# Output projection in pairs of token tiles with seven block products, in a bidirectional RWKV-7 / short-convolution layer

## The chip, the cores and the metric

One of the eight cores of a Trainium2 chip runs the whole kernel. The metric is the device time of one execution in microseconds (us). Five engines work beside each other: TensorE (PE, matrix products), VectorE (DVE), ScalarE (ACT), GpSimd (POOL) and SyncE (SP, whose queue issues the DMAs). Each engine takes its instructions in the order in which they stand in its own row, and an instruction that waits holds back all that stand behind it in that row.

## The reference, cut to what matters

128 context tokens and 2048 latent tokens of width 1024 go through one layer. Group A (512 channels) is RWKV-7 mixing with one scan in each direction, group B (512 channels) a gated short convolution. What the change touches is the end:

```python
    ya, s_final = _wkv(h, r, k, v, s0, lp)
    ya = ya.astype(x.dtype) * jax.nn.silu(g_a)
    yb = b_gate * _short_conv(c_gate * u_conv, lp['conv_w'], is_latent) * jax.nn.silu(g_b)
    u = jnp.concatenate([ya, yb], axis=-1) @ lp['w_out']
    return x + gate * u, s_final
    ...
    y_sample = _rmsnorm(lat, final_g)
```

So each token's 1024 mixed channels are multiplied by the 1024 x 1024 matrix `w_out`, scaled by a gate, added to x and normalised over the 1024 outputs. All is float32.

## The kernel before, in words

The program has three phases on one timeline. Phase 1 makes the input projection, phase 2 the two scans (17 stages; a stage handles one pair of heads and 512 tokens in each direction), phase 3 the output projection. The order of PE, DVE and ACT around the end of the scan is written out by hand as a long list of words, `LATE` (line 766): a word such as `S20@16` names a step and the stage or token tile that it is for, and `main` (line 1386 on) runs the list word by word. The rows of POOL and SP are set by a scheduler.

**Phase 3.** The mixed channels of all tokens lie in DRAM as `scr_mixT` (channel, token). The tokens are cut into 17 tiles of 128, in the order `TILES` (5 to 12, 0, 13 to 16, 1 to 4: the last scan stage finishes the tiles 13 to 16 and 1 to 4). `w_out` is kept in SBUF as eight blocks of 128 rows, four for the convolution's channels (`CONV`) and four for the scan's (`ATT`), each split in a high part `woh` and a low part `wol` (`w_high`, `w_low`). A product of full float32 precision is made of three matmuls in the reduced type fp32r: high by high, high by low, low by high (`products`, line 1499). For each tile the kernel does the following.

- It loads the tile's 8 blocks of 128 channels in two DMAs (`m_load`, line 1479: `mxc`, `mxa`), rounds them to the high part on ACT (`m_high`, line 1490) and subtracts to get the low part on DVE (`m_low`, line 1496: `mlc`, `mla`).
- For each half h of the 1024 outputs it sums 8 blocks x 3 matmuls of 128 x 512 in one PSUM bank: `conv_part` and `att_part` (words `P`, `B`). In matmuls that is 17 tiles x 2 halves x 24 = 816. For the first three tiles (`AHEAD`) the convolution's half is made first, into `psa`, and set aside in `z0` (`ahead`, line 1507, `ahead_out`).
- DVE multiplies the bank by the gate (`gated`, lines 1559 to 1562, word `Z`), POOL adds x (`added`, line 1568, word `G`), ACT squares and sums (`squares`, line 1576, `Q`), DVE adds the two sums (`square_sum`, line 1580, `ss`), ACT takes the root (line 1583, `rt`), DVE the inverse (line 1586, `rc`) and the scaled output (`out`, line 1591, `fo`), which SP stores.

**The end of the scan.** The last stage, 16, has eight state steps for each direction: `state` (line 1220, words `S00` to `S71`: four matmuls `psS<-sv,E`), then `scaled` (line 1246, `sv`: DVE scales the new state and puts it where the next step reads it). So step i+1 needs the `sv` of step i. `outputs` (line 1265) takes the results out, and `finish` normalises them and writes the last quarter of the scan's channels of eight tiles to `scr_mixT`. Before, these steps stand far apart: between two of them are 12 matmuls of the projection of tiles that are ready.

## Time and profile before

| | us |
|---|---|
| median of three runs | 1581.75 (1580.43 to 1589.68) |
| profiled execution, first to last instruction (span) | 1578.3 |
| first matmul of the projection starts | 1371.26 |
| last matmul of the projection starts | 1570.30 |
| granted TensorE clock, mean | 0.982 |

The own device time of the profiled execution is not shown beside its span, so the text takes the median less the span, 3.45 us, for what lies around it. In the profile, "busy" is the time in which an engine executes; "idle before, releaser" is the time that it stood just before an instruction and what ended it. Matmul durations overlap in a pipeline, so the rate is read from how many fit in a stretch and not from one duration. L1568 is line 1568 of the kernel. Tile names stand without their numbers in the profile: `z<-psu,gb` writes a `z` tile from a `psu` bank and the gate.

### The profile page before, as it was taken

The numbers are of one execution on the slowest core, as the hardware profiler recorded it, in microseconds if no ns is written. First come the engines' busy times: TensorE is split into PE (matmuls) and PEld (weight loads), VectorE is DVE, ScalarE is ACT, GpSimd is POOL, SyncE is SP. The second block draws the span as 40 slices with busy tenths as digits, with TensorE's granted clock in tenths as the row PEclk, the third lists the DMA queues.
The fourth block names the chain that finished last, engine by engine and source line by source line (L and its number), as shares of the span: only waits on it lengthen the run. The fifth ranks groups of instructions, "written<-read, shape, count | busy, mean of one in ns | idle before, by whom it ended". The sixth has DMA issues, their size and how long they took to land.

```text
span 1578.3 us, 39371 instructions
## 1 busy us (share of the span) xinstructions
...
## 2 busy tenths in 40 slices
...
GB/s 371 213 174 264 269 270 332 223 223 115 225 220 217 233 226 180 145 116 233 261 218 267 194 125 178 150 188 159 194 192 179 193 163 149 180 142 188 151 143 93
DMA packets 204579, 313.78 MB, mean 199 GB/s; under 512 B 58088, under 2 KB 147560, under 8 KB 190320
## 3 DMA queue, kind: packets, MB, share of 16 engines
...
## 4 chain that ended last, share of the span: by engine, by line
PE 65%; DVE 14%; POOL 7%; issue 5%; DMA 5%; ACT 2%; SPq 0%; ACTq 0%; DVEq 0%; POOLq 0%
POOL zt L1094 4%; PE psu L1503 4%; PE psu L1504 4%; PE psu L1505 4%; PE psE L1189 3%; POOL ztmp L1091 3%; PE mmb L182 2%; PE mmb L184 2%; PE mmb L183 2%; PE psS L1220 2%; PE mmc L182 2%; PE mmc L184 2%; PE mmc L183 2%; PE mmu L182 2%; PE mmu L184 2%
## 5 line engine op out<-in xcount | busy, mean ns | idle before, releaser
L1094 POOL TENSOR_TENSOR zt<-zt,ztmp 128x30 f32<-128x30 f32 (+7 forms) x510 | 215.4, 422 | 39.8
L1091 POOL TENSOR_TENSOR ztmp<-ab,zt 128x60 f32<-128x60 f32 (+7 forms) x255 | 139.4, 547 | 66.7 <-DVE ab L1082 47.0
L410 POOL TENSOR_TENSOR sh<-rawl 128x384 f32<-128x384 f32 (+1 forms) x48 | 47.5, 1007 | 210.1 <-ACT rawl L401 210.1
L1220 PE MATMUL psS<-sv,E 128*64 128x64 f32 x2176 | 104.6, 229 | 12.8 <-DVE sv L1246 7.3
L1220 PEld LDWEIGHTS psS<-sv,E 128*64 128x64 f32 x2176 | 82.8, 137 | 37.9 <-issue 16.3
L1194 DVE TENSOR_TENSOR E<-psE,msk 128x512 f32<-128x512 f32 x136 | 90.6, 683 | 20.0 <-PE psE L1189 18.9
L1568 POOL TENSOR_TENSOR z<-z,x 128x512 f32<-128x512 f32 x32 | 42.7, 1337 | 147.6 <-DVE z L1562 85.7
L1175 ACT ACTIVATE stf<-psX 64x512 f32<-64x512 f32 x136 | 80.3, 590 | 13.1 <-PE psX L1171 10.7
L434 POOL TENSOR_TENSOR hsl<-sq,hsh 128x384 fp32r<-128x384 f32 (+1 forms) x24 | 34.1, 1421 | 129.9 <-ACT hsh L429 121.6
L1246 DVE TENSOR_TENSOR sv<-psS,pc 64x128 f32<-64x128 f32 x254 | 63.7, 271 | 22.4 <-PE psS L1220 21.7
L182 PE MATMUL mmg<-h,w 128*128 128x384 f32 (+1 forms) x216 | 70.8, 328 | 0.0
L183 PE MATMUL mmg<-h,w 128*128 128x384 f32 (+1 forms) x216 | 70.7, 327 | 0.0
L184 PE MATMUL mmg<-h,w 128*128 128x384 f32 (+1 forms) x216 | 70.7, 327 | 0.0
L219 POOL TENSOR_TENSOR hslq<-ssq,hshq 128x384 fp32r<-128x384 f32 (+1 forms) x4 | 4.8, 1202 | 174.2 <-ACT hshq L218 109.6
L182 PE MATMUL mmb<-h,w 128*128 128x384 f32 (+1 forms) x192 | 63.9, 333 | 4.0 <-DMA w<-scr_wsp 4.0
L182 PE MATMUL mmv<-h,w 128*128 128x384 f32 (+1 forms) x192 | 63.1, 329 | 0.9 <-DVE sg L524 0.6
L184 PE MATMUL mmc<-h,w 128*128 128x384 f32 (+1 forms) x192 | 62.8, 327 | 1.0 <-DVE w L154 1.0
L184 PE MATMUL mmb<-h,w 128*128 128x384 f32 (+1 forms) x192 | 63.7, 332 | 0.0
L183 PE MATMUL mmb<-h,w 128*128 128x384 f32 (+1 forms) x192 | 63.6, 331 | 0.0
L182 PE MATMUL mmu<-h,w 128*128 128x384 f32 (+1 forms) x192 | 63.0, 328 | 0.2
L182 PE MATMUL mmc<-h,w 128*128 128x384 f32 (+1 forms) x192 | 63.0, 328 | 0.0
L184 PE MATMUL mmu<-h,w 128*128 128x384 f32 (+1 forms) x192 | 62.9, 328 | 0.0
...
## 6 DMA issues: line engine op xcount, KB each, us to landing
...
wr<-in_win SPq DMA_DIRECT2D x34, 512.0 KB, 8.2
x<-in_x SPq DMA_DIRECT2D x17, 512.0 KB, 3.9
...
```

The source lines that it names most:

```text
L182: T.matmul(ps[:, :n], w[:, 0, k], hh[:, 0, k, :n], start=k == 0, stop=False)
L183: T.matmul(ps[:, :n], w[:, 0, k], hh[:, 1, k, :n], start=False, stop=False)
L184: T.matmul(ps[:, :n], w[:, 1, k], hh[:, 0, k, :n], start=False, stop=k == 7)
L1091: G.tensor_tensor(tv, ab[:, j:j + 2, j + 2:32].unsqueeze(1).broadcast_to((128, kn, 2, n)), zt[:, :kn, j:j + 2].unsqueeze(3).broadcast_to(( ...
L1094: G.tensor_tensor(zt[:, :kn, j + 2:32], zt[:, :kn, j + 2:32], tv[:, :, r], ALU.subtract)
L1175: P.activation(g.fs[64:128, :, hd, e::2], g.ps["X"][e][hr_].rearrange("p a (b t) -> p b a t", b=2), AF.Copy, scale=-1.0)
L1194: V.tensor_tensor(g.E[n][:, k:k + 2].rearrange("p a b c -> p (a b) c"), pe[:].rearrange("p a b c -> p (a b) c"), B.msk[:, ME[g.d]].unsquee ...
L1220: T.matmul(g.sp[i // 4][r, q, hd, :], g.E[n][:, k, hd, r], g.sv[:, u, hd, :], start=True, stop=True)
L1246: V.tensor_tensor(dst, g.sp[i // 4][0:64, q], B.pc[0:64, d, 2 * p:2 * p + 2, c:c + 1].broadcast_to((64, 2, 64)), ALU.mult)
L1503: T.matmul(ps[:], mh[:, n], hi[:, cs], start=start and n == 0, stop=False)
L1504: T.matmul(ps[:], mh[:, n], lo[:, cs], start=False, stop=False)
L1505: T.matmul(ps[:], ml[:, n], hi[:, cs], start=False, stop=stop and n == 3)
```

## The change

**Three tiles** (5, 6, 7) stay as they were (`SINGLE`), and only tile 5 makes its convolution half first, in pieces of three matmuls (`A10` to `A03`). **The other 14 tiles** are taken in seven pairs (`TWO`). The two tiles of a pair (256 tokens) are seen as a 2 x 2 block matrix: two tiles by two halves of the channels (`K1`, `K2`). `w_out` is a 2 x 2 block matrix too: two halves of channels by two halves of outputs. Seven products of blocks with sums before and after (the Winograd form of Strassen's method) replace eight. A block product is 4 blocks x 3 matmuls of 128 x 512, as before. Before, a pair has 8 x 12 = 96 matmuls, now 7 x 12 = 84; in all there are 732 and not 816.

Around the products there is new work.

- *Once* (`vL`, `t1` to `t4`, `tH`, `tD`): `w_out` is loaded a second time in 12 DMAs; DVE makes 16 sums of 128 x 512, ACT rounds 16, and of the 16 low parts DVE makes 8 and POOL 8. Four of the results replace old blocks of `w_out`, which waits for the last matmul of tile 7 that reads them.
- *For each pair*, one pair ahead: a 512 KB load per tile, and seven left operands: a11, a12 and a22 as loaded, and the sums s3, s1, s2, s4 on POOL (`left_sum`), written over the loaded tile; each is rounded on ACT (`H`) and its low part made on DVE (`D`). Before there were four such operands for two tiles.
- *After the products*: ACT copies the first bank (`EX`), DVE makes seven sums of a bank and an SBUF tile (`E2`, `C11`, `E3`, `C22`, `E4`, `C12`, `C21`) and, in four of these words, a multiplication by the gate of two SBUF tiles. Before it was one multiplication straight from the bank for each half tile, four for two tiles. For the last two tiles DVE adds x and the output goes out in halves.

**The scan's last stage** has its state steps next to each other, both directions by turns, with three matmuls of tile 5 between two steps. Some tiles (`sg`, `w`, `q` of one block) get buffers of their own. The left pool of the scan is closed sooner, since the new right operands lie there.

The diff, cut:

```diff
-    AHEAD = TILES[:3]
+    SINGLE = TILES[:3]
+    TWO = [(a, b) for a, b in zip(TILES[3::2], TILES[4::2])]
+    K1, K2 = (0, 1, 4, 5), (2, 3, 6, 7)
...
-            (V if i == TILES[-1] else G).tensor_tensor(zs[i][:, cs], zs[i][:, cs], xs[i][:, cs], ALU.add)
+            (V if i in TILES[-2:] else G).tensor_tensor(zs[i][:, cs], zs[i][:, cs], xs[i][:, cs], ALU.add)
...
+    def again(j):
+        vr = raws["v", j] = K.spare(6 + j % 2, f"wa{j}", F32), K.small("zt", f"wb{j}"), K.small(("Q00", "Q01", "Q10", "Q11")[j], f"wc{j}")
...
+    def right_sum(n):
+        def f(j):
+            o = right_raw(n, j)
+            x, y = {1: (right_raw(3, j), o), 3: (right_raw(2, j), o), 2: (o, right_raw(1, j)), 4: (o, right_raw(2, j))}[n]
+            V.tensor_tensor(o, x, y, ALU.subtract)
+        return f
+
+    def right_high(n):
+        def f(j):
+            P.copy(tw[n][j][0][:], right_raw(n, j))
+        return f
+
+    def right_low(n):
+        def f(j):
+            hi, lo = tw[n][j]
+            (G if n % 2 else V).tensor_tensor(lo[:], right_raw(n, j), hi[:].bitcast(F32), ALU.subtract)
+        return f
+
+    def both_load(q):
+        for t, i in zip("ab", TWO[q]):
+            mx = raws[t, q] = O.r.tile([128, 8, 128], F32, tag="raw", name=f"m{t}{q}", bufs=2)
...
+    def left_sum(n):
+        def f(q):
...
+            x, y, op = dict(s3=("a11", "s1", ALU.subtract), s1=("s1", "a22", ALU.add), s2=("a22", "s3", ALU.subtract),
+                            s4=("a12", "s2", ALU.subtract))[n]
+            G.tensor_tensor(left_raw(n, q), left_raw(x, q), left_raw(y, q), op)
+        return f
...
+    def left_high(n):
+        def f(q):
+            left_tiles(n, q)
+            P.copy(four(lw[n, q][0]), left_raw(n, q))
+        return f
+
+    def left_low(n):
+        def f(q):
+            V.tensor_tensor(four(lw[n, q][1]), left_raw(n, q), four(lw[n, q][0]).bitcast(F32), ALU.subtract)
+        return f
...
+    ORDER = (1, 6, 2, 7, 5, 3, 4)
+
+    def seventh(n):
+        def f(q):
+            c, nm = (q * 7 + ORDER.index(n)) % 4, f"psw{n}_{q}"
+            ps = pss[n, q] = (O.pr if c == 1 else O.pl).tile([128, 512], F32, tag="u", name=nm) if c % 2 else K.bank(nm)
+            mh, ml = lw[LEFT[n], q]
+            for j in range(4):
+                hi, lo = right(n, j)
+                T.matmul(ps[:], mh[:, j], hi, start=j == 0, stop=False)
+                T.matmul(ps[:], mh[:, j], lo, start=False, stop=False)
+                T.matmul(ps[:], ml[:, j], hi, start=False, stop=j == 3)
+        return f
...
+    def plus(n, src, dst, gate=False):
+        def f(q):
+            z, gb = part(q, *dst)
+            V.tensor_tensor(z, pss[n, q][:], part(q, *src)[0], ALU.add)
+            if gate:
+                V.tensor_tensor(z, z, gb, ALU.mult)
+        return f
...
+C11@5 G0@1 Hs2@6 Ds2@6 Q0@1 M5@5 E3@5 Ha12@6 Da12@6 s4@6 M3@5 C22@5 G1@2 Q1@2 E4@5 Hs1@6 Hs3@6 Ds1@6 Ds3@6
+M4@5 C12@5 G1@1 Hs4@6 Ds4@6 Q1@1 ss@1 rt@1 rc@1 fo@1 M1@6 C21@5 G0@2 Ha22@6 Da22@6 Q0@2 ss@2 rt@2 rc@2 fo@2
```

**How the rows move.** Up to the last matmuls `psE` of stage 16 the rows of PE, DVE and ACT hold the same instructions in the same order; SP has eight of the new loads among the scan's.

*DVE at the end of the scan, before* (`psS` is the bank of a state step, `sv` the state scaled for the next step, `E` an operator of a step, `y` the result of the context tokens, `ymn` and `yss` its mean and square sum):

```order
L1246 TENSOR_TENSOR sv_16807<-psS_0_0_17489,pc 64x128
L1265 TENSOR_TENSOR y_17468<-psS_1_0_17236,y_17468 64x512
L1265 TENSOR_TENSOR y_17468<-psS_1_4_17349,y_17468 64x512
L1292 TENSOR_REDUCE ymn_17553<-y_17468 128x8
L1293 SCALAR_TENSOR_TENSOR y_17468<-ymn_17553,y_17468 128x512
L1194 TENSOR_TENSOR E_1738_17441<-psE_16_1739_17443,msk 128x512
L1301 TENSOR_REDUCE yss_17575<-w_17573 128x8
L1246 TENSOR_TENSOR sv_17018<-psS_1_0_17497,pc 64x128
L1194 TENSOR_TENSOR E_1740_17452<-psE_16_1745_17506,msk 128x512
```

*DVE at the same place, now:*

```order
L1252 TENSOR_TENSOR sv_16807<-psS_0_0_17501,pc 64x128
L1200 TENSOR_TENSOR E_1738_17441<-psE_16_1739_17443,msk 128x512
L1252 TENSOR_TENSOR sv_17018<-psS_1_0_17509,pc 64x128
L1200 TENSOR_TENSOR E_1740_17452<-psE_16_1745_17518,msk 128x512
L1271 TENSOR_TENSOR y_17480<-psS_1_0_17236,y_17480 64x512
L1271 TENSOR_TENSOR y_17480<-psS_1_4_17349,y_17480 64x512
L1298 TENSOR_REDUCE ymn_17567<-y_17480 128x8
L1299 SCALAR_TENSOR_TENSOR y_17480<-ymn_17567,y_17480 128x512
L1252 TENSOR_TENSOR sv_16807<-psS_0_0_17501,pc 64x128
L1252 TENSOR_TENSOR sv_17018<-psS_1_0_17509,pc 64x128
```

The two operators moved ahead of the four instructions on `y`, and the second state of both directions follows right behind them.

*DVE in the projection, before, one token tile* (`z` is the tile's result, `psu` its bank, `mlc` and `mla` the low parts of a coming tile, `ss` the square sum):

```order
L1562 TENSOR_TENSOR z_18700<-psu_0_18645,gb 128x512
L1496 TENSOR_TENSOR mlc_18716<-mxc_18643,mhc_18715 128x512
L1496 TENSOR_TENSOR mla_18738<-mxa_18663,mha_18737 128x512
L1562 TENSOR_TENSOR z_18700<-psu_1_18687,gb 128x512
L1580 TENSOR_TENSOR ss_18718<-ss_18718 128x1
L1586 RECIPROCAL ss_18718<-ss_18718 128x1
L1591 SCALAR_TENSOR_TENSOR z_18700<-z_18700,ss_18718,fg 128x1024
```

*DVE in the projection, now, a stretch of the second pair* (`zw` are the results of its two tiles, `psw` a bank of a block product; `s2r` holds s2, `ma` and `mb` the loaded tiles of the third pair, `mls` and `mla` low parts of its left operands). It begins with the word `C11` and ends before the last low part of s4:

```order
L1728 TENSOR_TENSOR zw_18252<-psw_1_18255,zw_18253 128x512
L1730 TENSOR_TENSOR zw_18252<-zw_18252,gb 128x512
L1689 TENSOR_TENSOR mls_2_18294<-s2r_18275,mhs_2_18293 128x512
L1728 TENSOR_TENSOR zw_18253<-psw_1_18277,zw_18252 128x512
L1689 TENSOR_TENSOR mla_2_18315<-ma_18231,mha_2_18314 128x512
L1728 TENSOR_TENSOR zw_18253<-psw_1_18300,zw_18253 128x512
L1730 TENSOR_TENSOR zw_18253<-zw_18253,gb 128x512
L1728 TENSOR_TENSOR zw_18252<-psw_1_18300,zw_18252 128x512
L1689 TENSOR_TENSOR mls_2_18340<-mb_18233,mhs_2_18339 128x512
L1689 TENSOR_TENSOR mls_2_18343<-ma_18231,mhs_2_18342 128x512
L1728 TENSOR_TENSOR zw_18252<-psw_1_18319,zw_18252 128x512
L1730 TENSOR_TENSOR zw_18252<-zw_18252,gb 128x512
```

The sums of a pair and the low parts for the next pair stand by turns in one row, and behind this stretch come `ss`, the reciprocal and the output of each tile, with the sum of the seventh product between the two tiles.

*POOL in the same pair, now* (before, POOL has only the two additions of x for each tile there):

```order
L1673 TENSOR_TENSOR ma_18231<-ma_18231,mb_18233 128x2x256
L1673 TENSOR_TENSOR mb_18233<-mb_18233 128x2x256
L1673 TENSOR_TENSOR s2r_18275<-mb_18233,ma_18231 128x512
L1591 TENSOR_TENSOR zw_18252<-zw_18252,x_18237 128x512
L1673 TENSOR_TENSOR ma_18231<-ma_18231,s2r_18275 128x2x256
L1591 TENSOR_TENSOR zw_18253<-zw_18253,x_18235 128x512
L1591 TENSOR_TENSOR zw_18252<-zw_18252,x_18237 128x512
L1591 TENSOR_TENSOR zw_18253<-zw_18253,x_18235 128x512
```

The three sums s3, s1 and s2 stand ahead of the first addition of x, and s4 between the first and the second. On ACT the squares of a half tile stand ahead of the roundings of a12 and of s1 for the next pair.

More of the change, by code (lines that the diff above doesn't have):

```diff
@@ L1417, in main, with small, bank @@
         O.pS.close()
-        for p in (O.l0, O.rI, O.r0):
+        for p in (O.rI, O.r0):
             p.close()
-    K.early, K.main, K.spare = early, main, spare
+    def small(tag, name, dt=F32):
+        return (O.rI if tag in ("zt", "dg") else O.r0).tile([128, 512], dt, tag=tag, name=name, bufs=2 if tag == "zt" else 1)
+    def bank(name):
+        return O.pS.tile([128, 512], F32, tag="S", name=name)
+    K.early, K.main, K.spare, K.small, K.bank = early, main, spare, small, bank
 def layout2(I):
@@ L1539, in f @@
         def f(i):
-            ps = pss[h, i] = getattr(O, pool).tile([128, 512], F32, tag="u", name=f"psu{i}_{h}")
+            nm = f"psu{i}_{h}"
+            ps = pss[h, i] = K.bank(nm) if pool == "pS" else getattr(O, pool).tile([128, 512], F32, tag="u", name=nm)
             if i not in z0:
@@ new lines, in left_tiles @@
+    def left_tiles(n, q):
+        x = dict(a11="a", a12="a", a22="c").get(n)
+        pool, b = ((O.r, 1) if x == "c" else (O.l, 2)) if x else (O.w, 1)
+        lw[n, q] = [pool.tile([128, 4, 128], F32R, tag=f"m{m}{x or n}", name=f"m{m}{n}_{q}", bufs=b) for m in "hl"]
+        return lw[n, q]
+    def left_sum(n):
+        def f(q):
+            if n == "s2":
+                raws["s2", q] = K.small("msk", f"s2r{q}")
+            x, y, op = dict(s3=("a11", "s1", ALU.subtract), s1=("s1", "a22", ALU.add), s2=("a22", "s3", ALU.subtract),
+                            s4=("a12", "s2", ALU.subtract))[n]
+            G.tensor_tensor(left_raw(n, q), left_raw(x, q), left_raw(y, q), op)
+        return f
```

147 lines of the change are left out of this document (101 added, 46 removed).

## The prediction

> **What bounds the kernel now.** I read the stages first, then what PE waited for, then the tail. The stages (start and end, length, busy time of PE, PEld, DVE, ACT and POOL with their instructions, granted clock, DMA share, GB/s):
>
> ```profile
> 1340.00:1380.00 40.00, 34.10 (x547) 27.88 (x544) 28.45 (x54) 23.14 (x38) 9.49 (x5) 0.97 0.58 171
> 1500.00:1540.00 40.00, 40.00 (x176) 32.85 (x175) 14.92 (x25) 10.51 (x25) 9.43 (x8) 1.00 0.42 138
> ```
>
> In the second, PE is busy without a gap while DVE works 14.92 of 40 us: 176 matmuls in 40.00 us are 0.2273 us each, 2.73 for a block product of 12. The waits of PE from 1384 to 1571 and the two ends of the projection:
>
> ```profile
> PE psa L1503 <- ACT mhc L1490: 2.1, 1, 2.1
> ...
> 1371.26 0.50 PE L1503 MATMUL psa<-woh,mhc 128*128 128x512 f32 x1
> ...
> 1570.30 0.39 PE L1505 MATMUL psu<-woh,mla 128*128 128x512 f32 x1
> ...
> 1573.71 1.42 DVE L1591 SCALAR_TENSOR_TENSOR z<-z,ss,fg 128x512 f32<-128x512 f32 x2
> ```
>
> One wait of 2.1 us in 199: PE alone sets the pace. DVE's last instruction ends at 1575.13, the span 3.2 us later.
>
> **What the change removes.** 816 matmuls become 732; 84 x 0.2273 = 19.1 us of PE, 2.73 for each pair (21.8 before, 19.1 now). This is the whole gain, 1.2% of 1578. Everything else that the change does costs time, if it isn't hidden under PE.
>
> **The vector engines in a pair.** The groups from 1430 us on (busy, mean ns | idle before):
>
> ```profile
> L1591 DVE SCALAR_TENSOR_TENSOR z<-z,ss,fg 128x1024 f32<-128x1024 f32 (+1 forms) x16 | 20.9, 1312 | 1.4
> L1562 DVE TENSOR_TENSOR z<-psu,gb 128x512 f32<-128x512 f32 x26 | 17.7, 685 | 13.8 <-PE psu L1505 8.4 <-DMA out_y<-z 5.3
> L1496 DVE TENSOR_TENSOR mlc<-mxc,mhc 128x512 fp32r<-128x512 f32 x12 | 8.3, 690 | 17.8 <-ACT mhc L1490 15.7 <-PE psT L1317 2.0
> L1580 DVE TENSOR_TENSOR ss<-ss 128x1 f32<-128x1 f32 x13 | 2.0, 157 | 20.1 <-ACT sq L1576 20.0
> ...
> L1490 ACT CAST mhc<-mxc 128x512 fp32r<-128x512 f32 x12 | 7.4, 620 | 37.0 <-PE psu L1504 37.0
> ...
> L1568 POOL TENSOR_TENSOR z<-z,x 128x512 f32<-128x512 f32 x24 | 31.5, 1314 | 105.2 <-DVE z L1562 84.5 <-DMA mxa<-scr_mixT 13.2 <-DVE ss L1580 5.2
> ```
>
> DVE's work for a pair, now: 7 sums from a bank, 4 multiplications by the gate and 7 low parts, 18 at about 0.69 = 12.4; two outputs at 1.29 = 2.6; four small ones at 0.16 = 0.6. Together 15.6 us, under PE's 19.1. If that were all, the change would gain. But DVE takes its row in order, and the row holds five places where it must wait for a chain over other engines. The price of such a chain stands in the last but one tile:
>
> ```profile
> 1559.74 0.69 DVE L1562 TENSOR_TENSOR z<-psu,gb 128x512 f32<-128x512 f32 x1 [1.39 <-PE psu L1505]
> 1560.51 1.29 POOL L1568 TENSOR_TENSOR z<-z,x 128x512 f32<-128x512 f32 x1 [4.16 <-DVE z L1562]
> 1561.83 0.64 ACT L1576 ACTIVATE sq<-z 128x512 f32<-128x512 f32 x1 [4.21 <-POOL z L1568]
> 1562.37 0.18 ACT L1576 ACTIVATION_READ_ACCUMULATOR sq<-z 128x1 f32 x1
> 1562.59 0.16 DVE L1580 TENSOR_TENSOR ss<-ss 128x1 f32<-128x1 f32 x1 [2.16 <-ACT sq L1576]
> 1562.78 0.29 ACT L1583 ACTIVATE ss<-ss,eps 128x1 f32<-128x1 f32 x1 [0.23 <-DVE ss L1580]
> 1563.11 0.16 DVE L1586 RECIPROCAL ss<-ss 128x1 f32<-128x1 f32 x1 [0.36 <-ACT ss L1583]
> 1563.38 1.29 DVE L1591 SCALAR_TENSOR_TENSOR z<-z,ss,fg 128x1024 f32<-128x1024 f32 x1
> ```
>
> DVE ends the gate at 1560.43 and can start the output at 1563.38: 2.95 us, in which it stood for 2.16 before `ss`. Before, this comes under 10.9 us of PE for each tile and costs nothing. The five waits of a pair, in the order of DVE's row:
>
> - Low part of s2. s3 is written over a11, so it waits for DVE's low part of a11; then POOL makes s3, s1 and s2 (3 x 1.29) and ACT rounds (0.62): 4.65 with the handovers. DVE has `C11` (1.4) in between and stands 3.2.
> - Low part of a12: its rounding stands on ACT behind the square of a half tile, 0.5.
> - Low part of s1: its rounding stands behind a square that waits for POOL's addition behind `C22`: 1.29 + 0.8 + 0.62 + 0.1 = 2.8, less `E4` 0.7: 2.1.
> - `ss` of the first tile: 2.95 less the low part of s4 (0.69) and the small ones (0.3): 1.95. `ss` of the second: 1.95 again.
>
> These are 9.7 us, so DVE needs 15.6 + 9.7 = **25.3 us for a pair** with no instruction slowed. Two things come on top. First, DVE and POOL get in each other's way:
>
> ```profile
> 1417.62 1.29 POOL L1568 TENSOR_TENSOR z<-z,x 128x512 f32<-128x512 f32 x1 [11.50 <-DVE z L1560]
> 1418.03 1.43 DVE L1560 TENSOR_TENSOR z<-z,gb 128x512 f32<-128x512 f32 x1
> ...
> 1420.18 0.67 DVE L1562 TENSOR_TENSOR z<-psu,gb 128x512 f32<-128x512 f32 x1
> ...
> 1421.84 1.36 DVE L1496 TENSOR_TENSOR mla<-mxa,mha 128x512 fp32r<-128x512 f32 x1
> ...
> 1488.72 2.33 DVE L1591 SCALAR_TENSOR_TENSOR z<-z,ss,fg 128x1024 f32<-128x1024 f32 x1
> ```
>
> A DVE instruction on two SBUF tiles that meets a POOL instruction ends 0.55 us after POOL's end (1418.91, 1419.46), and so takes 1.43 or 1.36 and not 0.69, the output 2.33 and not 1.29; one on a bank and one SBUF tile takes 0.67 beside POOL all the same. In a pair the gates, low parts and outputs are of the first kind and POOL has eight instructions and not four. Where two meet (the gates of `C11` and `C22`, the low part of s2, the last addition of either tile) 0.5 to 0.75 us are lost, of which some fall into waits: +1.6 a pair, from 0 to 2.5. The Trainium skill states this as a rule: by its page "SBUF — State Buffer", section "Who interferes with whom", DVE with two SBUF inputs and a GpSimd instruction that reads SBUF exclude each other for a whole instruction, whichever is first. By that rule a pair is 27 us and without it 25.3; the rows above agree with it (1.43 against 0.67).
>
> Second, the loads. On SP's queue the second tile of the pair after next stands behind a load of x that waits for POOL's last addition of this pair, about 3 us before DVE's next pair begins:
>
> ```profile
> x<-in_x SPq DMA_DIRECT2D x11, 512.0 KB, 3.4
> ```
>
> s3 needs the tile 1.4 us into that pair, so 4.4 us are there: one load is in time, two behind each other are late by up to 1.8. I count 0.1: **27.0 us a pair, from 25.3 to 29**. PE's 19.1 lie under it: its products of a pair need the low parts that DVE made a pair before, so PE follows DVE's row and is idle for about 8 us of 27. The eight banks don't hold it up; each is emptied before its next product is due.
>
> **The scan's end.** PE's own work from 1371.26 to the first product of tile 5 with the scan's channels is 24 matmuls (5.5), 56 of state steps (0.45 for 8: 3.2) and four transposes (0.6): 9.3 us. What the steps wait for stands in DVE's row:
>
> ```profile
> 1372.11 1.40 DVE L1265 TENSOR_TENSOR y<-psS,y 64x512 f32<-64x512 f32 x2
> 1373.54 0.69 DVE L1292 TENSOR_REDUCE ymn<-y 128x8 f32<-128x512 f32 x1
> 1374.26 0.69 DVE L1293 SCALAR_TENSOR_TENSOR y<-ymn,y 128x512 f32<-128x512 f32 x1
> ...
> 1376.30 0.27 DVE L1246 TENSOR_TENSOR sv<-psS,pc 64x128 f32<-64x128 f32 x1
> ```
>
> The third step stands behind the four `y` instructions (2.8 us) and finds about 0.3 of cover: 2.5. Each later step needs its `sv` (0.27 twice), and DVE has 9 longer instructions between them against 0.68 of matmuls a step: 3 us more. So 14.8, until 1386.0; from 9.3 to 18.
>
> **From there to the first sum of the first pair.** DVE has 64 instructions in its row: 53 of about 0.70 (37.1), three outputs (3.9), eight small ones (1.4): 42.4 us. They contain the 16 sums of blocks of `w_out` and eight low parts. The waits: the last `y` (square, root, transposes) 3; s2 behind three POOL sums 4.6; the four new blocks of `w_out`, whose roundings stand behind a square of tile 7, 2.7; a12 behind another, 2.7; s4 1.9; three outputs 1.5. That is 16.4. POOL makes eight low parts for which there is a price:
>
> ```profile
> 1364.33 4.71 POOL L1477 TENSOR_TENSOR wol<-woraw,woh 128x1024 fp32r<-128x1024 f32 x2 [17.71 <-ACT woh L1473]
> ```
>
> 1.18 for 512 elements, 9.4 in all, in a stretch where DVE works almost only on pairs of SBUF tiles; 4 of it fall into DVE's waits: +5.4, from 0 to 9. Together 64.2 us, from 58 to 70. PE has 30 us of work here and stands the rest.
>
> **The last pair and the tail.** There are no low parts for a next pair. 15 instructions at 0.69 (10.4), four half outputs (2.8), small ones 0.6, two waits for `ss` of 1.25 and the final store 3.2: 19.5 us. The eight extra loads of `w_out` among the scan's (2.5 MB) stand on SP where their buffers come free; the scan waits for DMAs little there and I cost them at nothing, at most 3 us.
>
> **The sum.** 1371.3 + 14.8 + 64.2 + 6 x 27.0 + 19.5 = 1631.8 us of span, 53.5 more than the profiled execution's 1578.3. The median of the runs lies 3.45 above that span, so **1635 us**, 3.4% slower. With all lower bounds 1371.3 + 9.3 + 58 + 151.8 + 18 = 1608.4, with the upper ones 1371.3 + 18 + 70 + 174 + 21 = 1654.3; in time 1612 and 1658.
>
> **Rivals.** *PE sets the pace of the pairs.* This is the way to no loss: it needs DVE's row at 19.1 or less, so that of 11.4 us of waits and meetings only 3.5 are left. For it: DVE's work alone is 15.6, and in the rows of before the wait for `ss` cost PE nothing. Against it: nothing in the row lets DVE do other work during those waits. Then the first pair still begins late, its last five products starting at about 1445 (1450.2 less 4.9 for s4 and an output): 1445 + 13.7 + 6 x 19.1 + 10.6 of tail (7.6 as before from the last matmul's end, and 3 since the other tile's chain stands ahead) = 1584, in time 1587; with the lower bounds of the two stages before it, 11.7 less, 1576. *The chains alone*, with no meeting on the port and no late load: 1371.3 + 14.8 + 58.8 + 151.8 + 19.5 = 1616.2, in time 1620. For it: DVE's instructions may fall where POOL has none. *The queue of SP*: with x late on every pair a pair takes 29: 1643.8, in time 1647. For it: SP's order; against it: 3.4 us of landing are short. *That the change doesn't do what it says:* PE's row has 84 matmuls fewer, so this is out.
>
> **How the numbers follow.** My forecast, 1635 (chains and meetings, 26 to 28 a pair), has 0.52; the chains alone, 1620, 0.17; the queue, 1647, 0.16; PE at the pace, 1576 to 1587, 0.12; a real gain (all waits hidden, also ahead of the pairs) 0.03. A measurement of this kernel tells about 1% (16 us) from no change. Faster by over 1% is the last case, 0.03; within 1% is PE at the pace, 0.12; slower by over 1% the other three, 0.85. The range leaves out PE's case and the far ends of the bounds: 1606 to 1655.
>
> **What would show it.** If I am right, the stage of the pairs shows PE busy some 70%, and PE's waits there are for DVE's low parts (`mls`, `mla`), most at s2 and s3; DVE waits 2 us before each `ss` for ACT, 3 before the low part of s2, 2 before that of s1; a pair takes 25 to 29 us from one `EX` to the next; between 1371 and 1386 PE waits for `sv`; and between about 1405 and 1445 PE stands 20 us or more. I am wrong if PE has no gaps between products of the pairs, if a pair takes 19 to 21 us, or if DVE's waits are there but short because POOL or ACT ran ahead.

## The result, and the profile after

| | before | after |
|---|---|---|
| median of the runs, us | 1582.18 (4 runs, 1580.43 to 1589.68) | 1646.69 (4 runs, 1646.27 to 1651.7) |
| span of the profiled execution, us | 1578.3 | 1645.0 |
| first matmul of the projection starts | 1371.26 | 1375.04 |
| last matmul of the projection starts | 1570.30 | 1623.88 |
| matmuls from the first on | 940 | 856 |
| granted TensorE clock, mean | 0.982 | 0.963 |

The ratio is 1.0408, 95% interval 1.0377 to 1.0439: 4.1% slower. PE has the 84 matmuls fewer that were announced, and needs 248.8 us and not 199.0 from the first to the last of them; behind the last one come 21.1 us and not 8.0; the first starts 3.8 us later. These three are the 66.7 us by which the spans differ.

The stages after (columns as in the prediction's table of stages: start and end, length, busy time of PE, PEld, DVE, ACT and POOL with their instructions, granted clock, DMA share, GB/s):

```profile
1371.00:1386.00 15.00, 12.02 (x138) 8.45 (x133) 12.02 (x26) 3.04 (x6) 1.91 (x2) 0.89 0.70 209
...
1400.00:1460.00 60.00, 40.21 (x145) 29.36 (x144) 43.47 (x53) 19.08 (x40) 26.52 (x18) 0.82 0.34 110
...
1514.00:1541.00 27.00, 22.78 (x88) 16.87 (x87) 16.79 (x26) 7.66 (x18) 11.38 (x9) 0.94 0.36 126
```

The middle row is the stretch ahead of the first pair: 145 matmuls in 60 us, where 264 would fit at 0.2273. The last row is a pair: 88 matmuls in 27 us where 119 would fit. DVE is busy for only 16.79 of them, so neither engine is full. What ends the waits in four pairs (1487 to 1594; us in total, times, longest):

```profile
DVE mls L1689 <- ACT mhs L1684: 20.4, 8, 3.0
...
DVE ss L1603 <- ACT sq L1599: 15.5, 8, 1.9
PEld psw L1711 <- ACT mhs L1684: 13.7, 6, 2.8
...
PEld psw L1713 <- DVE mls L1689: 5.0, 8, 0.8
```

DVE waits twice a pair for a rounded sum (20.4 / 4 = 5.1 us a pair) and twice for a tile's squares (3.9 us a pair). PE waits for the operands that come out of that chain. One pair on DVE's row (start, duration, and in brackets the idle time before and what ended it):

```profile
1520.69 1.34 DVE L1730 TENSOR_TENSOR z<-z,gb 128x512 f32<-128x512 f32 x1
1525.07 1.09 DVE L1689 TENSOR_TENSOR mls<-s2r,mhs 128x512 fp32r<-128x512 f32 x1 [3.04 <-ACT mhs L1684]
...
1528.25 1.33 DVE L1730 TENSOR_TENSOR z<-z,gb 128x512 f32<-128x512 f32 x1
...
1532.24 0.69 DVE L1689 TENSOR_TENSOR mls<-mb,mhs 128x512 fp32r<-128x512 f32 x1 [2.06 <-ACT mhs L1684]
...
1537.40 0.16 DVE L1603 TENSOR_TENSOR ss<-ss 128x1 f32<-128x1 f32 x1 [1.95 <-ACT sq L1599]
...
1543.36 0.16 DVE L1603 TENSOR_TENSOR ss<-ss 128x1 f32<-128x1 f32 x1 [1.94 <-ACT sq L1599]
```

and the copy `EX` that begins a pair, on ACT, in two pairs behind each other:

```profile
1517.18 0.57 ACT L1723 COPY z<-psw 128x512 f32<-128x512 f32 x1
...
1543.75 0.57 ACT L1723 COPY zw<-psw 128x512 f32<-128x512 f32 x1
```

A pair takes 26.57 us. The four long waits are 3.04, 2.06, 1.95 and 1.94; the fifth of the prediction (low part of a12) is 0.15. Three instructions of 0.69 take 1.34, 1.33 and 1.09. Each of them began while one of these instructions of POOL was running:

```profile
1520.19 1.29 POOL L1673 TENSOR_TENSOR ma<-ma,mb 128x512 f32<-128x512 f32 x1 [4.20 <-DVE mla L1689]
1524.35 1.27 POOL L1591 TENSOR_TENSOR z<-z,x 128x512 f32<-128x512 f32 x1
1527.76 1.27 POOL L1673 TENSOR_TENSOR ma<-ma,s2r 128x512 f32<-128x512 f32 x1 [2.14 <-DVE mla L1689]
```

POOL's three end at 1521.48, 1525.62 and 1529.03, DVE's at 1522.03, 1526.16 and 1529.58: 0.54 or 0.55 us later each time, however long the two had lain beside each other.

### The profile page after: what moved, and what is told of

The parts are those of the page before. It is cut to its first block, busy times and chain, and to the rows that moved or that the text cites. A ratio compares the mean times of both kernels' runs of the same rounds, so it can differ in the third digit from the quotient of the medians.

```text
span 1645.0 us, 39402 instructions
## 1 busy us (share of the span) xinstructions
PE 1507.8 (92%) x16124; PEld 1376.0 (84%) x16124; DVE 1214.6 (74%) x2050; ACT 792.9 (48%) x1502; POOL 620.8 (38%) x996
## 4 chain that ended last, share of the span: by engine, by line
PE 49%; DVE 15%; POOL 15%; issue 8%; DMA 7%; ACT 4%; SPq 1%; ACTq 0%; POOLq 0%; DVEq 0%
POOL zt L1100 6%; POOL ztmp L1097 4%; PE psE L1195 3%; PE mmb L182 2%; PE mmb L184 2%; PE mmb L183 2%; PE mmc L182 2%; PE mmc L184 2%; PE mmc L183 2%; PE mmu L184 2%; PE mmgb L183 2%; PE mmu L182 2%; PE mmgb L184 2%; PE mmu L183 2%; PE mmgb L182 2%
## 5 line engine op out<-in xcount | busy, mean ns | idle before, releaser
L1100 POOL TENSOR_TENSOR zt<-zt,ztmp 128x30 f32<-128x30 f32 (+7 forms) x510 | 212.0, 416 | 39.8
L1226 PEld LDWEIGHTS psS<-sv,E 128*64 128x64 f32 x2176 | 83.7, 140 | 44.7 <-DVE sv L1252 21.1
L1200 DVE TENSOR_TENSOR E<-psE,msk 128x512 f32<-128x512 f32 x136 | 90.7, 683 | 20.0 <-PE psE L1195 18.4
L183 PE MATMUL mmg<-h,w 128*128 128x384 f32 (+1 forms) x216 | 70.7, 327 | 0.0
L182 PE MATMUL mmb<-h,w 128*128 128x384 f32 (+1 forms) x192 | 62.8, 327 | 1.4 <-DMA w<-scr_wsp 1.4
L182 PE MATMUL mmv<-h,w 128*128 128x384 f32 (+1 forms) x192 | 63.0, 328 | 1.1 <-DVE sg L524 1.1
L184 PE MATMUL mmc<-h,w 128*128 128x384 f32 (+1 forms) x192 | 62.8, 327 | 1.0 <-DVE w L154 1.0
L182 PE MATMUL mmc<-h,w 128*128 128x384 f32 (+1 forms) x192 | 63.0, 328 | 0.0
L184 PE MATMUL mmb<-h,w 128*128 128x384 f32 (+1 forms) x192 | 62.7, 327 | 0.0
L184 PE MATMUL mmv<-h,w 128*128 128x384 f32 (+1 forms) x192 | 62.6, 326 | 0.0
L183 PE MATMUL mmc<-h,w 128*128 128x384 f32 (+1 forms) x192 | 62.6, 326 | 0.0
```

The source lines that it names most:

```text
L182: T.matmul(ps[:, :n], w[:, 0, k], hh[:, 0, k, :n], start=k == 0, stop=False)
L183: T.matmul(ps[:, :n], w[:, 0, k], hh[:, 1, k, :n], start=False, stop=False)
L184: T.matmul(ps[:, :n], w[:, 1, k], hh[:, 0, k, :n], start=False, stop=k == 7)
L1100: G.tensor_tensor(zt[:, :kn, j + 2:32], zt[:, :kn, j + 2:32], tv[:, :, r], ALU.subtract)
L1200: V.tensor_tensor(g.E[n][:, k:k + 2].rearrange("p a b c -> p (a b) c"), pe[:].rearrange("p a b c -> p (a b) c"), B.msk[:, ME[g.d]].unsquee ...
L1226: T.matmul(g.sp[i // 4][r, q, hd, :], g.E[n][:, k, hd, r], g.sv[:, u, hd, :], start=True, stop=True)
```

## The experiments

Times are set against before by the ratio, since each kernel was timed beside runs of before, which lay between 1573 and 1593 us.

| run | ratio to before | median, us | from one `EX` to the next, later pairs |
|---|---|---|---|
| the change | 1.0408 (1.0377 to 1.0439) | 1646.69 | 26.6 |
| e5_no_prep | 1.0225 (1.0200 to 1.0250) | 1613.04 | 26.6 |
| e6_fin_later | 1.0392 (1.0359 to 1.0426) | 1641.16 | 26.6 |
| e13_other_buffers | 1.0392 (1.0360 to 1.0424) | 1643.71 | 26.6 |
| e1_out_later | 1.0341 (1.0316 to 1.0366) | 1631.27 | 24.9 to 25.3 |
| e2_left_later | 1.0289 (1.0266 to 1.0312) | 1624.48 | 23.6 to 23.7 |
| e7_both_sp | 1.0224 (1.0192 to 1.0255) | 1614.90 | 21.2 to 22.7 |
| e8_both_x_dve | 1.0228 (1.0194 to 1.0262) | 1614.93 | 20.8 to 21.2 |
| e12_all_dve | 1.0186 (1.0146 to 1.0226) | 1608.89 | 20.9 to 21.2 |
| e10_no_pool | 1.0076 (1.0046 to 1.0107) | 1588.48 | 19.4 |
| e11_no_pairs | 1.0018 (0.9994 to 1.0043) | 1581.79 | none |
| e9_seven_singles | 1.0060 (1.0038 to 1.0082) | 1590.24 | 22.0 to 22.5 |
| e14_seven_singles_dve | 1.0018 (0.9998 to 1.0038) | 1583.52 | 20.9 |

**The theory.** DVE's row, taken in order, sets the end: ahead of the first pair by its work on the right operands, in the pairs by waits for chains over POOL and ACT, and in both by meetings with POOL. The rivals: the meetings alone, late loads, and the state steps at once.

### The right operands left out

```diff
-... Lw@0 G0@5 P0l@6 t1@0 t3@0 t2@0 t4@0 vL@2 tH1@0 tH3@0 tH2@0 tD1@0 tD3@0 tD2@0 AH@7 ...
+... Lw@0 G0@5 P0l@6 AH@7 ...
-            return [t_[:] for t_ in tw[n - 4 if n < 7 else 3][j]]
+            return [w[:, HALF[0]] for w in wk[K1[j]]]
```

> The second load of w_out and its 16 sums, 16 roundings and 16 low parts are left out; the products that need them take old blocks of w_out, so the output differs. Theory (DVE's row sets the stage from the scan's end to the first sum of the first pair, and the right operands are its greatest part): DVE's 24 instructions for them last 26 us in the trace of after, with the waits in them 29, so the first sum comes 25 to 32 us sooner; the 2.5 MB of loads among the scan's are gone, so the first matmul of tile 5 comes 2 to 4 us sooner. Pairs stay at 26.5. Kernel 1647 - 32 = 1615 (1611 to 1620). Rival (the stage is set by the chains of the three single tiles and of the first left operands, and the right ones lie beside them): only 5 to 15 us sooner, 1632 to 1642.

Measured: 1.8% less, 29 us. From the first product of tile 5 with the scan's channels to the first sum of the first pair it is 43.4 us and not 70.7, so 27.3 of the 25 to 32 expected. The stage's busy times (1394 to 1437):

```profile
1394.00:1437.00 43.00, 42.76 (x189) 34.30 (x188) 23.70 (x39) 14.54 (x33) 13.55 (x10) 1.00 0.51 167
```

PE has 189 matmuls in 43 us, 0.2275 each: it doesn't stand, and DVE needs 23.70. So what made PE stand there is DVE's work on the right operands, as the theory has it. One part of the expectation fell: the first matmul of the projection starts at 1376.5 without the extra loads and at 1375.0 with them. In the other kernels with the same rows up to there it lies between 1368.8 and 1383.2. So no cost of the loads shows there, and the 3.8 us are within what differs from run to run.

### The scan's finish behind the state steps

```diff
-... T@15.1 S50@16 S51@16 sv50@16 sv51@16 fy@15.1 fa@15.1 A01@5 S60@16 S61@16 ... A03@5 AE0@5 AH@6 ...
+... T@15.1 S50@16 S51@16 sv50@16 sv51@16 A01@5 S60@16 S61@16 ... A03@5 AE0@5 fy@15.1 fa@15.1 AH@6 ...
```

> One step of the scan's finish (the words fy and fa of stage 15, the second direction), which multiplies by tiles that are loaded late, is moved from between the sixth and seventh state step to behind the last one. Theory (DVE stands 2.5 and 1.0 us there for two loads, with the state's next step behind it in its row): the first product of tile 5 with the scan's channels comes 13 to 16 us after the first matmul of tile 5 and not 19.9; of this some 3 to 5 us reach the end, 1643. Rival (the state steps' own round trip or the y instructions set the stage): it stays at 18 to 20 us and the kernel within 1 us.

In the change, this is DVE's row between the sixth and the last state step:

```profile
1389.98 1.12 DVE L1328 SCALAR_TENSOR_TENSOR sg<-psT,gwh,sg 128x128 f32<-128x128 f32 x4 [2.46 <-DMA sg<-scr_sg]
1392.11 0.69 DVE L1330 TENSOR_TENSOR sg<-sg,w 128x512 f32<-128x512 f32 x1 [1.00 <-DMA w<-scr_q]
1392.72 0.47 DVE L1252 TENSOR_TENSOR sv<-psS,pc 64x128 f32<-64x128 f32 x2
```

and in the experiment:

```profile
1387.02 0.52 DVE L1252 TENSOR_TENSOR sv<-psS,pc 64x128 f32<-64x128 f32 x2 [0.99 <-PE psS L1226]
1387.46 0.68 DVE L1516 TENSOR_TENSOR mla<-mxa,mha 128x512 fp32r<-128x512 f32 x1
1388.06 1.11 DVE L1328 SCALAR_TENSOR_TENSOR sg<-psT,gwh,sg 128x128 f32<-128x128 f32 x4
```

The last `sv` no longer stands behind two late loads, and by the time that their tiles are needed they have landed. The first product of tile 5 with the scan's channels comes 15.7 us after the first matmul of tile 5 and not 19.9: the theory's 13 to 16. The 4.2 us between these two profiles are not all the move's doing. In the ten profiles with the old order the two waits for loads are 1.0 to 3.8 us together and the stage takes 16.8 to 20.1, 18.4 in the mean; in the three with the move it takes 15.7 to 15.9. That is 2.7 us. The ratio falls by 0.16%, 2.5 us, just below the 3 to 5 expected and too little to be told from nothing by the time alone.

### The first pair's buffers

DVE's row of the change has a wait that the prediction did not have:

```profile
1460.44 1.28 DVE L1614 SCALAR_TENSOR_TENSOR z<-z,ss,fg 128x1024 f32<-128x1024 f32 x1
1465.60 0.69 DVE L1728 TENSOR_TENSOR z<-psw,z 128x512 f32<-128x512 f32 x1 [3.87 <-DMA out_y<-z]
```

```diff
-            zs[i] = K.spare(6 + t, f"zw{i}", F32) if q % 2 else tl([128, 1024], "z", i)
+            zs[i] = K.spare(6 + t, f"zw{i}", F32) if q % 2 == 0 else tl([128, 1024], "z", i)
```

> As the changed kernel, with one thing other: the results of the first, third, fifth and seventh pair lie in the buffers that had belonged to the second, fourth and sixth, so that the first pair does not take over the buffers of tiles 6 and 7. Nothing is left out. Theory (in the trace of after DVE stands 3.9 us before the first sum of the first pair until tile 7's output is stored, a wait that the prediction did not have): the first sum follows the copy EX by 1.6 us and not 5.5, the first pair takes 26.6 to 27 us and not 30.5, pairs stay at 26.6, and the kernel gains 3 to 4 us. Rival (another wait lies just behind it, PE's products of that pair at half the clock): less than 1.5 us.

```profile
1454.91 1.28 DVE L1614 SCALAR_TENSOR_TENSOR z<-z,ss,fg 128x1024 f32<-128x1024 f32 x1
1456.11 0.68 DVE L1728 TENSOR_TENSOR zw<-psw,zw 128x512 f32<-128x512 f32 x1
```

The first sum follows tile 7's output at once. `EX` to the first sum is 1.5 us and not 5.5, as the theory had it; the first pair takes 27.5 us and not 30.5, just above the 26.6 to 27 expected. The ratio fell by 0.16%, 2.5 us, a little under the 3 to 4 expected, and as before the time alone would not show it.

### The outputs later

A pair's words, before and after (the pair of tiles 12 and 0):

```diff
-M7@2 C11@2 G0@12 ... Hs4@3 Ds4@3 Q1@12 ss@12 rt@12 rc@12 fo@12 M1@3 C21@2 G0@0 Ha22@3 Da22@3 Q0@0 ss@0 rt@0 rc@0 fo@0
+M7@2 C11@2 ss@11 rt@11 rc@11 fo@11 G0@12 ... Hs4@3 Ds4@3 Q1@12 M1@3 C21@2 G0@0 Ha22@3 Da22@3 ss@12 rt@12 rc@12 fo@12 Q0@0
```

> The four words that end a tile (ss, rt, rc, fo) are moved back in the rows of the pairs: those of the first tile behind the low part of a22, those of the second behind C11 of the next pair. POOL's row in the pairs is written in the order that it had. Nothing is left out. Theory (DVE's row in order, with waits for chains over POOL and ACT): both waits of 1.95 us before ss go, and the 2.1 us of the second tile's ss, rc and fo now lie in the 3.0 us before the low part of s2, so a pair falls from 26.5 to about 20.5 us (20 to 22) and the kernel by 30 to 38 us, to about 1612. Rival (DVE is held up by POOL on the port, whatever the order): the same instructions meet, a pair stays at 25.5 to 26.5 and the kernel within 6 us of 1647. Rival (loads on SP are late): a pair stays at 26.5 or becomes longer, and DVE or POOL wait for ma or mb.

Measured: 24.9 to 25.3 us a pair and 0.7% less time, a third of what the theory said and more than either rival. Both waits before `ss` went, as expected, but the wait before the low part of s2 grew from 3.04 to 4.39 in spite of the four words now ahead of it. POOL's row and DVE's row of one pair, and SP's row with the loads for the next:

```profile
1511.64 1.86 POOL L1673 TENSOR_TENSOR ma<-ma,mb 128x512 f32<-128x512 f32 x1 [6.68 <-DMA mb<-scr_mixT]
```

```profile
1516.74 1.09 DVE L1689 TENSOR_TENSOR mls<-s2r,mhs 128x512 fp32r<-128x512 f32 x1 [4.39 <-ACT mhs L1684]
```

```profile
1528.33 2.25 SPq L1558 DMA_DIRECT2D x<-in_x  x2
1530.79 0.38 SPq L1655 DMA_DIRECT2D mb<-scr_mixT  x1
```

The scheduler that sets SP's row put the load of `mb` behind both loads of x, and one of these waits for POOL's last addition. So `mb` landed 2.9 us after DVE had released s3. The theory held for the waits that were moved, and the late load, a rival of the prediction, took their place.

### The left operands later

```diff
-M7@2 C11@2 G0@12 Hs2@3 Ds2@3 Q0@12 M5@2 E3@2 Ha12@3 Da12@3 s4@3 M3@2 C22@2 G1@0 Q1@0 E4@2 Hs1@3 Hs3@3 Ds1@3 Ds3@3 M4@2
+M7@2 C11@2 G0@12 Ha12@3 Da12@3 s4@3 M5@2 E3@2 M3@2 C22@2 G1@0 Hs2@3 Ds2@3 Q0@12 E4@2 Hs1@3 Hs3@3 Ds1@3 Ds3@3 Q1@0 M4@2
```

> Only the left operands are moved: the rounding and low part of s2 stand behind C22 and no longer behind C11, a12 stands ahead of them, and ACT's squares behind the roundings of s2, s1 and s3. The outputs stay where they were. Theory (waits in DVE's row): the 3.0 us before the low part of s2 and the 2.1 us before that of s1 go, the two of 1.95 us before ss stay, so a pair falls from 26.5 to about 21.5 us (21 to 23) and the kernel by 24 to 33 us, to about 1618. Rival (meetings with POOL on the port): no change beyond 1 us a pair, the kernel within 6 us of 1647. Rival (late loads): no change, DVE waits elsewhere for the same time.

Measured: 23.6 to 23.7 us a pair, above the theory's 21 to 23, and 1.2% less time, 19 us in place of 24 to 33. The waits before the low parts of s2 and s1 are gone. They were 5.1 us, and the pair became 2.9 shorter. The rest is in the durations, here on DVE and POOL:

```profile
1511.72 1.78 DVE L1689 TENSOR_TENSOR mla<-ma,mha 128x512 fp32r<-128x512 f32 x1
...
1514.92 1.53 DVE L1730 TENSOR_TENSOR z<-z,gb 128x512 f32<-128x512 f32 x1
1516.38 1.76 DVE L1689 TENSOR_TENSOR mls<-s2r,mhs 128x512 fp32r<-128x512 f32 x1
...
1518.66 1.18 DVE L1689 TENSOR_TENSOR mls<-mb,mhs 128x512 fp32r<-128x512 f32 x1
```

```profile
1511.32 1.62 POOL L1673 TENSOR_TENSOR mb<-mb 128x512 f32<-128x512 f32 x1
1512.90 1.75 POOL L1673 TENSOR_TENSOR s2r<-mb,ma 128x512 f32<-128x512 f32 x1
```

While DVE waited, POOL's work met nothing. Now DVE works in that time, and both get longer: five DVE instructions (a gate just before these, of 1.33, and the four shown) lose 0.6, 1.1, 0.8, 1.1 and 0.5 us, 4.1 a pair in place of 1.7. Theory and rival both hold a part: the waits were the price, and nearly half of it is given back in meetings.

### Both moves, with SP's row

```diff
+ENG = ("PE", "DVE", "Activation", "Pool", "SP")
-M4@2 C12@2 G1@12 ... Q1@12 ... M1@3 C21@2 G0@0 Ha22@3 Da22@3 Q0@0 ... mL@4 xL@14 xL@13
+M4@2 C12@2 G1@12 Hs4@3 Ds4@3 mLa@4 Q1@12 xL@13 M1@3 C21@2 G0@0 Ha22@3 Da22@3 mLb@4 xL@14 ss@12 rt@12 rc@12 fo@12 Q0@0
```

> Both moves together, outputs later and left operands later, and in the pairs SP's row is written too: the load of ma stands behind the low part of s4, that of mb behind the low part of a22, each x directly behind the addition that frees its buffer. Nothing is left out. Theory (waits in DVE's row, then meetings on the port): the four waits of 9 us are covered; DVE has 15.6 us of work and, as where the left operands were moved alone, about 4 us of meetings with POOL, so a pair takes 19.5 to 21 us, the kernel 1646.7 - 6 x 6.2 = 1609 (1602 to 1614). Rival (late loads, which took back 4.4 us a pair where the outputs alone were moved): POOL still waits for mb and a pair stays at 23 to 25 us. Rival (PE sets the pace once the waits are gone): 19.1 to 19.4 us and PE without gaps, 1601.

Measured: 21.2 to 22.7 us a pair, 1614.9 us, 1.8% less than the change: just above the theory's range. In the pair from 1506 to 1527 DVE waits 0.75 us for one low part and 1.2 in all for the small steps around the root; its busy time is 19.12 of 21.4, with 4.7 us of it in meetings. POOL still waits for `mb` in that pair, and its first sum starts 1.7 us after DVE has released the tile, but DVE no longer waits for what follows. SP's new row also cost something at one place: tile 7's store now stands behind the loads of x, and the first sum of the first pair waits for it 7.2 us.

### POOL taken out of the pairs

```diff
-            G.tensor_tensor(left_raw(n, q), left_raw(x, q), left_raw(y, q), op)
+            return
...
```

> Both moves and SP's row as in e7_both_sp, and POOL has no work in the pairs: the four sums of left blocks and the additions of x are left out for the 14 tiles (the products take the blocks as loaded), so the output differs. Theory (what is left over DVE's work in that kernel, 21.2 to 21.8 us a pair, is meetings with POOL): DVE's row falls to about 17 us, PE sets the pace with 84 matmuls at 0.2273, a pair takes 19.1 to 19.8 us and the kernel 1601 (1596 to 1607). Rival (DVE's row itself, its handovers and small instructions, needs 21): a pair stays at 20.5 to 21.5 us, 1611 to 1615.

```profile
1490.00:1511.00 21.00, 21.00 (x93) 17.11 (x92) 15.29 (x26) 8.75 (x20) 0.00 (x0) 1.00 0.48 166
```

Measured: 19.4 us a pair, PE without a gap, 93 matmuls in 21 us (0.2258 each), and 1588.5 us: below the 1596 to 1607 expected. With the meetings went a backlog that the sum did not have: PE had run ahead during the wait for the first sum and the first two pairs take 12.5 and 16 us. The verdict is in the stage: without POOL the same DVE row is short enough and PE is the bound; from 1490 to 1570 DVE waits 17.9 us for PE's banks. The edit takes away the chains over POOL as well as the meetings, but with both moves only about 2 us of waits a pair were left, against 4.7 of meetings.

> Both moves and SP's row as in e7_both_sp, and all eight POOL instructions of a pair, four sums and four additions of x, are on DVE. Nothing is left out. Theory (a POOL instruction shuts out DVE's instructions on two SBUF tiles for its whole length, so it costs about what DVE itself would need): no meetings, but 8 x 0.69 = 5.5 us more on DVE, 17 + 5.5 = 22.5, a pair at 21 to 23 us and the kernel within 8 us of 1615. Rival (POOL is the cause and DVE has room): 19.1 to 20 us a pair, 1602 to 1607.

```diff
-            G.tensor_tensor(left_raw(n, q), left_raw(x, q), left_raw(y, q), op)
+            V.tensor_tensor(left_raw(n, q), left_raw(x, q), left_raw(y, q), op)
-            (V if i in TILES[-2:] else G).tensor_tensor(zs[i][:, cs], zs[i][:, cs], xs[i][:, cs], ALU.add)
+            (V if i in TILES[3:] else G).tensor_tensor(zs[i][:, cs], zs[i][:, cs], xs[i][:, cs], ALU.add)
```

```profile
1490.00:1511.00 21.00, 21.00 (x93) 17.11 (x92) 19.74 (x33) 7.55 (x18) 0.00 (x0) 1.00 0.44 151
```

In DVE's row the three sums s3, s1 and s2 stand behind `C11` and the second tile's output. Measured: 20.9 to 21.2 us a pair, at the low end of the theory's 21 to 23, and 1608.9 us, within the 8 us of 1615 that it gave. DVE is busy 19.74 of 21 us, and eight more instructions on it cost no more than POOL's eight did beside it.

> The same as with both moves, and x is added on DVE and not on POOL for the 14 tiles in pairs. Nothing is left out. Theory (with the waits covered, what is left over DVE's own work is meetings with POOL): POOL has four instructions a pair and not eight, so about 2 us of meetings go, and DVE gets 4 x 0.69 = 2.8 us of work: a pair within 1 us of that with both moves. Rival (DVE's row was bound by its own work alone): 2.8 us a pair longer, 17 us in all. Rival (the additions on POOL cost in chains, not meetings): faster by 1 us a pair or more.

The second of the two edits of e12_all_dve, with the sums on POOL: 20.8 to 21.2 us a pair, 1614.9 us, the same as with both moves. Three ways to share the work (eight, four or none of the instructions on POOL) thus give 20.8 to 22.7 us. A POOL instruction costs DVE about what DVE would need for it: 4.7 us of meetings for eight, against 8 x 0.69 = 5.5.

### The scan's end alone, and fewer pairs

`SINGLE = TILES`, `TWO = []` and a list of single tiles behind the scan's end of the change:

> The scan's end of the change with all 17 tiles single: no second load of w_out, no pairs, 816 matmuls. Nothing is left out. Theory (the states at once cost PE 5 to 11 us of standing, since it has work of one tile there and not of three): 1580 + 8 = 1588 (1584 to 1593). Rival (the states at once cost nothing, all is lost in the pairs and ahead of them): 1578 to 1582. Rival (the scan's end is a great part of the loss): over 1600.

Measured: 1581.79, 0.18% over before, -1 to +7 us by the interval. The waits of PE from 1375 to 1400 and the two stages:

```profile
PE psS L1226 <- DVE sv L1252: 6.0, 2, 3.7
```

```profile
1378.00:1398.00 20.00, 13.67 (x148) 9.39 (x145) 14.07 (x34) 2.36 (x5) 0.00 (x0) 0.94 0.72 240
1398.00:1581.00 183.00, 183.00 (x799) 149.43 (x798) 78.53 (x129) 48.67 (x119) 43.33 (x30) 1.00 0.42 139
```

PE does stand 6.0 us for `sv`. From the first to the last matmul it is 203.0 us against 199.0 before, with as many matmuls. So the states at once cost about 4 us, less than the 5 to 11 that I expected; the longer of the two waits, 3.7 us, is behind the two late loads, which come here too. The time lies where the first rival had it (1578 to 1582) and doesn't tell the 4 us from nothing; that the scan's end is a great part of the loss is out. Behind it, 799 matmuls in 183 us leave no gap.

Seven single tiles and five pairs:

```diff
-    SINGLE = TILES[:3]
-    TWO = [(a, b) for a, b in zip(TILES[3::2], TILES[4::2])]
+    SINGLE = TILES[:7]
+    TWO = [(a, b) for a, b in zip(TILES[7::2], TILES[8::2])]
```

> Seven tiles stay single and five pairs follow, with both moves in the pairs, the scan's finish behind its state steps, and the first pair's results in other buffers than the last single tiles'. The second load of w_out and its sums, roundings and low parts are spread over the single tiles. Nothing is left out; 756 matmuls of the projection and not 732. Theory (the stage from the scan's end to the first pair is lost to DVE's work on the right operands while PE stands): with 48 more matmuls per two tiles of ready work there PE stays busy, seven tiles take 7 x 10.9 = 76 us less what lies before, pairs 5 x 20.5, the tail about 14: span 1390 + 72 + 102 + 14 = 1578, time 1573 to 1588, equal to before within 1%. Rival (DVE can't carry the preparation beside the single tiles either, 4.7 us a tile and 26 for the preparation, with meetings): singles take 13 us each and the time is 1590 to 1605.

Measured: 1590.24, 0.6% over before, at the border of theory and rival. The single tiles hide the right operands nearly whole (346 matmuls in the 84 us ahead of the first pair), but a pair takes 22.0 to 22.5 us, and two single tiles are 96 x 0.2273 = 21.8: the pairs gain nothing.

> Seven single tiles and five pairs as in e9_seven_singles, with the pairs' sums of left blocks and additions of x on DVE, as in e12_all_dve. Nothing is left out. Theory (a pair costs 22.3 us with POOL's work and 20.9 without its meetings; two single tiles cost 21.8): five pairs are 5 to 7 us shorter than in e9_seven_singles, the kernel 1583 to 1586, within 1% of before and not faster by more than the interval. Rival (the ratio of before is reached or passed): under 1576.

Measured: 1583.52, ratio 1.0018 (0.9998 to 1.0038), as the theory said: the pairs at 20.9 gain 0.9 us each, and the longer tail (12.4 us from the last matmul to the end, 8.0 before) and the scan's end take it back. No version beat the kernel before.

## Why the prediction was right, and which steps of it were off

The forecast was 1635 and slower with 0.85; it came to 1646.7, inside 1606 to 1655. The pairs, the main term, were right. Both stages ahead of them came out above their own upper bounds, 18 and 70. Term by term, on the span:

| term | predicted | measured |
|---|---|---|
| first matmul of the projection | 1371.3 | 1375.0 |
| to the first product of tile 5 with the scan's channels | 14.8 | 19.9 |
| to the first sum of the first pair | 64.2 | 70.7 |
| six pairs | 162.0 | 159.9 |
| last pair and tail | 19.5 | 19.5 |
| span | 1631.8 | 1645.0 |

To the span the forecast added 3.45 us, the median of before less one span. The runs that show both have 1.8 (1646.77 against 1645.0).

- **The pairs** were right in size and in cause. Four of the five waits of DVE were within 0.2 us of the forecast (3.2, 2.1, 1.95 and 1.95); the fifth was 0.15 and not 0.5. Meetings were 1.7 and not 1.6. That these waits are a great part of the price was shown by moving the words: the waits that were covered went, and the pair fell by 2.9 us with the left operands later and by 3.9 to 5.4 with both moves, of 9.0. What the prediction had not weighed is that a wait and a meeting exclude each other: while DVE stands, POOL's work is free. So the pace of PE, 19.1 us, the first rival, was not reached by covering waits (21.2 to 22.7, with 2 us of waits left); 19.4 was reached, but only without POOL's work.
- **The scan's end.** The step that was off is PE's own work, put at 9.3 us with "56 of state steps (0.45 for 8: 3.2)". PE stood 5.8 us in this stage, so its own work was 14.1. The profile has 16 matmuls for a step of both directions, 112 in all:

```profile
1379.57 0.69 PE L1226 MATMUL psS<-sv,E 128*64 128x64 f32 x16 [2.06 <-DVE sv L1252]
1381.74 1.12 PE L1226 MATMUL psS<-sv,E 128*64 128x64 f32 x16
1386.50 0.69 PE L1226 MATMUL psS<-sv,E 128*64 128x64 f32 x16
1388.02 0.69 PE L1226 MATMUL psS<-sv,E 128*64 128x64 f32 x16
1393.05 0.69 PE L1226 MATMUL psS<-sv,E 128*64 128x64 f32 x16 [3.45 <-DVE sv L1252]
```

  A step and its three matmuls of tile 5 take 1.52 us (1386.50 to 1388.02) where the prediction has 1.13; with the rest that is about 3 us. Another 1.8 went where the granted clock was low (0.56 from 1381 to 1384). The standing of 5.8 us is near the 5.5 of the prediction, but in part by luck. The wait behind the `y` instructions was 2.06 against 2.5. The 3 us for DVE's longer instructions between the later steps didn't come; in their place came 3.45, most of it for two late loads of the finish, with `sv` behind them. So "the scan waits for DMAs little there" was off for these two, and it isn't the extra loads of `w_out` that made them late: without these they cost DVE 1.7 us in e5_no_prep and 3.7 in e11_no_pairs. With the finish moved away the stage took 15.7 us, of which PE stood 2.2.
- **To the first sum.** The waits added up to 17.1 us (4.68, 3.09, 2.65, 2.41, 2.10, 1.06 and three roots of 0.36), against 16.4 predicted. Two sizes were off. The meetings with POOL's eight low parts were put at 5.4, at most 9. DVE's row and POOL's row there:

```profile
1411.08 1.81 DVE L1638 TENSOR_TENSOR wb<-wb,wa 128x512 f32<-128x512 f32 x1
1412.93 1.65 DVE L1638 TENSOR_TENSOR wc<-wc,wb 128x512 f32<-128x512 f32 x1
1414.50 0.68 DVE L1649 TENSOR_TENSOR tw2l<-wb,tw2h 128x512 fp32r<-128x512 f32 x1
```

```profile
1411.05 1.29 POOL L1649 TENSOR_TENSOR tw1l<-wa,tw1h 128x512 fp32r<-128x512 f32 x1 [1.88 <-ACT tw1h L1643]
1412.30 1.74 POOL L1649 TENSOR_TENSOR tw3l<-wa,tw3h 128x512 fp32r<-128x512 f32 x1
```

  Ten sums of this kind took 1.64 to 1.82 us and not 0.69, 10.2 us in all. Eight of them met a low part on POOL (8.2 us), two an addition of x (2.0), for which the sum had no term. DVE has no waits there under which POOL's instructions could fall. And the store of tile 7 (3.87 us) was no term at all, though the change's row of buffers shows that the first pair takes those of the last single tiles. Together 8.7 us more than allowed for; the rest of the stage was 2.2 us shorter. The sign that PE would stand 20 us or more between 1405 and 1445 was not met: it stood 11.7 there, and 8.0 in one stop that ended at 1456.
- **The loads.** No cost of the extra loads of `w_out` ahead of the projection shows in e5_no_prep, as the prediction had it. SP's queue, a rival at 0.16, did not decide in the change: in the four pairs no engine waited for `ma`, `mb` or x. It was near all the same, as the run with later outputs showed. For the prediction's "late by up to 1.8", two landings of 3.4 us in turn, less 4.4, would give 2.4.
- **Meetings with POOL.** From 1400 us on, 29 of DVE's instructions on two SBUF tiles (128 x 512) begin in the change while an instruction of POOL is running. Each ends 0.54 or 0.55 us after POOL's. It is the same for all 41 in e2_left_later and all 48 in e7_both_sp. The other way round, 27 of POOL's in the change begin during such an instruction of DVE, and each ends 1.12 to 1.16 us after it, where one takes 1.26 to 1.30 alone. DVE's sums of a bank and an SBUF tile are not held up: 41 of them in those two experiments begin while POOL is at work and take 0.67 to 0.69 us. So in a meeting one engine stands until the other's instruction is done, save for some 0.15 us. By this rule, which the prediction takes from the Trainium skill (page "SBUF — State Buffer", section "Who interferes with whom"), the pair would be 27 us, without it 25.3; 26.57 agrees with the rule. In time e12_all_dve and e10_no_pool show the same: 21.0 us a pair with POOL's share on DVE, 19.4 without it, 21.2 to 22.7 with it on POOL.

How PE follows DVE was told a little wrong: it ran nearly a pair ahead of DVE's sums and took each operand as soon as its low part was made (`tw2h,mhs` at 1525.09, with the sum s2 rounded at 1524.42), not a pair later. So PE's waits in the four pairs are mostly for ACT's roundings (12.2 us) and less for DVE's low parts (5.0), the other way round than the prediction's sign. For the pace it is the same.
